# Index products of the sampled tokens as eight tiles at a time, and flags found without TensorE

## The chip, the cores and the metric

The kernel runs on one NeuronCore of a Trainium2 chip. A core has five engines that run side by side, each through its own queue in order: TensorE (PE, with weight loads shown apart as PEld), VectorE (DVE), ScalarE (ACT), GpSimd (POOL) and SyncE (SP, which issues most of the DMAs). They wait for each other through semaphores. PE writes into PSUM banks of 128 rows by 512 float32; every other working buffer lies in SBUF. The metric is the time of one execution on the device in microseconds (us).

## The reference

One decoder step for 1024 prompt positions and, beside them, 8 sampled sequences of 4 new tokens each (32 rows), which have 8192 positions in a paged cache. A projection feeds two groups of heads: sparse attention, which looks only at the 256 keys per query that an indexer picks, and retention. A gated output projection, a norm and a gated embedding follow. The change concerns the indexer:

```python
def _index_select(qi, wi, ki, qpos, kpos, topk):
    s = jnp.einsum('bqhd,bsd->bqhs', qi, ki) * (D_IDX ** -0.5)
    score = jnp.einsum('bqh,bqhs->bqs', wi, jax.nn.relu(s))
    score = jnp.where(valid, score, -jnp.inf)
    top_val, top_idx = lax.top_k(score, topk)
    return top_idx, jnp.isfinite(top_val)
```

There are 8 index heads of 64 numbers. For the sampled sequences, the keys `ki` are gathered from the cache pages; for each sequence 8192 keys meet 4 tokens x 8 heads = 32 query columns.

## The kernel before, in words

The program runs in stages: norms and index projections with the prompt's index scores (to about 186 us), the sample index stage (to about 343), four loops over pairs of heads, in which retention's projections `pqk` and `pvg` run among attention pieces (to about 690), then prompt attention, output projection, gate and embedding. The order of instructions on each engine isn't written out by hand. A planner places them, by its own estimate of when each can run, from the order of the source and from generators that other loops step.

**The sample index stage** is the loop over `b` (8 sequences) and `a` (2 halves of the pages). For each `(b, a)`, POOL gathers 128 rows of keys (`kx`, L794). PE transposes them in two halves of eight 128x128 blocks (`ptx`, L804), and ACT copies each half out of PSUM (`kT`, L805, two buffers). Two keys lie in the 128 rows of a transposed column, 64 rows each. So `qbd` holds the queries as a block diagonal matrix, 128 rows by 64 columns: rows 0 to 63 with the 32 query columns of one key and zeros, rows 64 to 127 with zeros and the same queries. Two products (L808) of 512 columns each fill one bank `pox`, and ACT writes its relu into `rl` (L811). `head_sum` multiplies four such `rl` by the head weights in four tiles of 32 columns (`py`, L767 and L770), and ACT copies it to `ys` (L772). `by_key` transposes `ys` (`pxt`, L779), and DVE copies it into the order of the keys (`xe`, L783), which a DMA stores.

PSUM in this stage has two pairs of banks ("S", for `ptx`), two banks "b" (`py` and the projection's `pb`) and two banks "t", which `pox`, `pxt`, the flag's `pfl` and others share.

**What else runs in the loop.** `unit(1.4)` steps the projection (`pb`, products L252 to L254 with 384 or 288 columns), which gives PE work between the index products. `tickb` counts steps of `bisect_prompt`, the search for the prompt's 256 best keys per query. Its counting steps use DVE (L656) and ACT (`js`, L652). Then DVE finds the largest of what remains (`lw`, L697). Then a flag tells if any row needs a further search (`anywhere`, then a branch, L706, whose body this execution's data skip), and last DVE builds the mask for six query blocks of 384 to 1024 columns (L715 to L731). `anywhere` is used a second time, with its branch at L962, by `bisect_sample`, the search for the sampled tokens, whose totals per step (`stot`, L871) PE sums from `sgn` (L909) during the loops over pairs of heads. `anywhere` sums its operand over the 128 rows with a PE product into `pfl` (L621), DVE compares the sum with zero (L623), and DVE loads it into a register (L624).

Of the kernel before, what the change touches and what calls it, by code (L numbers as in the profile page):

```python
# [10 lines left out]
F32 = mybir.dt.float32  # L11
F32R = mybir.dt.float32r
BF16 = mybir.dt.bfloat16
I32 = mybir.dt.int32
# [106 lines left out]
def tile_step(ctx: ExitStack, tc: tile.TileContext, I, O):  # L121
    nc = tc.nc
# [176 lines left out]
    xt_d = dram.tile([8, 128, 512], F32, name="xt_d")  # L299
    wi_d = dram.tile([1, 256], F32, name="wi_d")  # L300
    def load_pt():
        ptp = lp
        pti = ptp.tile([128, 2, 8], I32, name="pti")
        pt_t = I["page_table"]
        for a in range(2):
            nc.sync.dma_start(pti[a::2, 0, :], pt_t.rearrange("b n -> n b"))
        nc.sync.dma_start(pti[:, 1, :], bass.AP(tensor=pt_t.tensor, offset=pt_t.offset + 63,
                                                  ap=[[0, 128], [64, 8]]))
        ptf = ptp.tile([128, 8], F32, name="ptf")
        nc.vector.tensor_copy(ptf, pti[:, 0, :])  # L310
        lf = ptp.tile([128, 8], F32, name="lf")
        nc.vector.tensor_copy(lf, pti[:, 1, :])
        nc.vector.tensor_scalar(lastidx, lf, 128.0, C("prow"), op0=ALU.mult, op1=ALU.add)
        kf = ptp.tile([128, 8], F32, name="kf")
        nc.vector.tensor_scalar(kf, ptf, 2.0, C("half"), op0=ALU.mult, op1=ALU.add)
        for a in range(2):
            nc.vector.tensor_scalar(kidx[:, a * 8:a * 8 + 8], kf, 2.0, float(a), op0=ALU.mult, op1=ALU.add)

        bi = ptp.tile([128, 2, 8], I32, name="bi")
        nc.vector.tensor_scalar(bi[:, 1, :], kf, 64.0, None, op0=ALU.mult)  # L320
        nc.vector.tensor_scalar(bi[:, 0, :], bi[:, 1, :], 11, 11, op0=ALU.arith_shift_right, op1=ALU.arith_shift_left)
        nc.vector.tensor_tensor(bi[:, 1, :], bi[:, 1, :], bi[:, 0, :], op=ALU.bitwise_xor)
        nc.vector.tensor_copy(base, bi)
# [31 lines left out]
    score = sp_.tile([128, NSC], F32, name="score")  # L355
    sxs = ExitStack()
    sx0 = sxs.enter_context(pool("sx0"))
    qbd = sx0.tile([128, 8, 64], F32, name="qbd")
    nc.gpsimd.memset(qbd, 0.0)
    kis = sx0.tile([64, NS], F32, name="kis")  # L360
    qsn = sx0.tile([64, 8, NS], F32, name="qsn")

    def q_sample_index(j, pt):
        for o in range(2):
            s = pt[o * 64:o * 64 + 64, 256:288].rearrange("p (b t) -> p b t", b=8)
            for r in range(2):
                d = qbd[r * 64:r * 64 + 64].rearrange("p b (r t h) -> p r b t h", r=2, h=8)
                nc.vector.tensor_scalar(d[:, r, :, :, 2 * j + o], s, 0.125, None, op0=ALU.mult)
            nc.vector.tensor_scalar(qsn[:, 2 * j + o, :], pt[o * 64:o * 64 + 64, 256:288], 0.125, None, op0=ALU.mult)


# [245 lines left out]

    def anywhere(bad, sp, name):

        t = bank("pfl", "t")  # L620
        nc.tensor.matmul(t[:1, :1], bad, sp_one, start=True, stop=True)  # L621
        fl = sp.tile([1, 1], I32, name=f"fl{name}")
        nc.vector.tensor_scalar(fl, t[:1, :1], 0.0, None, op0=ALU.is_gt)  # L623
        return nc.vector.value_load(fl)  # L624

    def bisect_prompt():

# [103 lines left out]
            V.tensor_scalar(mask[:, o:o + n], gt[:, :n], -BIG, BIG, op0=ALU.mult, op1=ALU.add)  # L731
            yield

    sp_one = cp.tile([128, 1], F32, name="sp_one")
    nc.gpsimd.memset(sp_one, 1.0)
    bp = bisect_prompt()

    def step(gen, n=1):
# [37 lines left out]
    def by_key(b, ys):  # L776
        pt = bank("pxt", "t")
        for i in range(4):
            nc.tensor.transpose(pt[:, i * 128:(i + 1) * 128], ys[:, i * 128:(i + 1) * 128], ident)  # L779
        xe = sx.tile([128, 4, 4, 4, 4], F32, tag="xe", bufs=1, name="xe")  # L780
        pv = pt.rearrange("p (r i e) -> p r i e", r=4, i=4)
        for t in range(4):
            nc.vector.tensor_copy(xe[:, t].rearrange("p i r u -> p r i u"), pv[:, :, :, t * 4:t * 4 + 4])  # L783
        nc.sync.dma_start(xs_d[:, b * 256:b * 256 + 256], xe.rearrange("p t i r u -> p (t i r u)"))

    def later():
        if pend:
# [2 lines left out]
    for b in range(8):  # L790
        rls = []
        for a in range(2):
            kx = sx.tile([128, 2048], F32, tag="kx", bufs=2, name="kx")
            nc.gpsimd.indirect_dma_start(  # L794
                out=kx, out_offset=None, in_=pages,
                in_offset=bass.IndirectOffsetOnAxis(ap=kidx[:, a * 8 + b:a * 8 + b + 1], axis=0))
            for up in range(2):
                pt = pair("ptx")
                kT = sx.tile([128, 1024], F32, tag="kT", bufs=2, name="kT")
                for u2 in range(2):  # L800
                    for i in range(4):
                        r2 = up * 8 + i * 2 + u2
                        c0 = u2 * 512 + i * 128
                        nc.tensor.transpose(pt[:, c0:c0 + 128], kx[:, r2 * 128:(r2 + 1) * 128], ident)  # L804
                nc.scalar.copy(kT, pt)  # L805
                po = bank("pox", "t")
                for u2 in range(2):
                    nc.tensor.matmul(po[u2 * 64:u2 * 64 + 64, :], qbd[:, b, :], kT[:, u2 * 512:u2 * 512 + 512],  # L808
                                     start=True, stop=True)
                rl = sx.tile([128, 512], F32, tag="rl", bufs=6, name="rl")  # L810
                nc.scalar.activation(rl, po, AF.Relu)  # L811
                rls.append(rl)
            later()
            tickb[0] += 1.5
            while tickb[0] >= 1:
                tickb[0] -= 1
                step(bp)
# [983 lines left out]
```

## Time and profile before

| what | value |
|---|---|
| time, median of 3 runs | 1080.16 us (1077.92 to 1082.97) |
| the profiled execution | 1081.17 us, its span 1079.4 us |
| PE busy | 999.9 us (93% of the span) |
| DVE busy | 698.3 us (65%) |
| ACT busy | 507.2 us (47%) |
| POOL busy | 287.9 us (27%) |

The profile shows one execution. "Busy" is the time in which an engine runs an instruction. A group's row gives the line, engine, operation, output and inputs, shapes, a count, and then either busy time and mean or the shortest, median and longest. What an engine waited for is named behind its idle time with an arrow. PEclk is the share of full clock that the throttle granted to PE.

### The profile page before, as it was taken

How to read it: one execution, taken by the hardware profiler on the slowest of the kernel's cores; microseconds unless marked ns; L12 is line 12 of the kernel's file. 1: busy time of each engine (PE TensorE's matmuls, PEld its weight loads, DVE VectorE, ACT ScalarE, POOL GpSimd, SP SyncE). 2: the span in 40 equal slices, each digit the busy share in tenths (PEclk: the TensorE clock that was granted, in tenths of full speed). 3: DMA queues.
4: the chain of work that ended last, by engine and by line, in shares of the span. 5: the costliest groups of instructions: out<-in, count | busy, mean ns of one | idle time of the engine just before them, and what ended most of it. 6: DMA issues, size and time to landing. Idle time of an engine off the chain costs nothing.

```text
span 1079.4 us, 19681 instructions
## 1 busy us (share of the span) xinstructions
PE 999.9 (93%) x7375; PEld 844.5 (78%) x7375; DVE 698.3 (65%) x2012; ACT 507.2 (47%) x1094; POOL 287.9 (27%) x287
## 2 busy tenths in 40 slices
PE   3899997988999889999889996999998799999998
PEld 2899997666776788898788884566665799999998
DVE  6847768989401898978967947776763522684332
ACT  5545554986434256842523436655554332452210
POOL 3102223111201532413713521635331321122100
PEclk9999999999999889999989995999999899999999
DMA  8211235546443211202201624524211511332211
GB/s 284 67 59 50 78 95 178 173 137 204 127 158 120 58 40 39 66 18 87 71 12 42 179 85 118 148 79 118 60 45 51 154 60 40 116 126 80 89 37 41
DMA packets 98309, 102.24 MB, mean 95 GB/s; under 512 B 21347, under 2 KB 88387, under 8 KB 95907
## 3 DMA queue, kind: packets, MB, share of 16 engines
q1 hardware_dynamic: 92450, 74.74, 23.1%
q0 software_dynamic: 5760, 26.22, 7.9%
q8 instruction: 58, 0.95, 0.4%
q14 instruction: 41, 0.33, 0.1%
HBM read 79.25 MB, written 21.68 MB: 94 GB/s over the span
## 4 chain that ended last, share of the span: by engine, by line
PE 65%; DVE 13%; issue 7%; ACT 6%; DMA 6%; POOL 3%; SPq 1%; DVEq 0%; POOLq 0%; ACTq 0%
PE pb L252 4%; PE pb L253 4%; PE pb L254 4%; PE pg L262 3%; PE pg L264 3%; PE pg L263 3%; PE po L262 2%; PE po L264 2%; PE po L263 2%; PE pvg L263 2%; PE pvg L264 2%; PE pvg L262 2%; PE ob L1577 2%; PE pox L808 2%; PE ptp L1569 2%
## 5 line engine op out<-in xcount | busy, mean ns | idle before, releaser
L1144 POOL DMA_INDIRECT kvs<-in_cache_kv,idx x64 | 66.1, 1032 | 92.0 <-ACT pT L1574 29.8
L262 PE MATMUL pqk<-whi_qkb,xh 128*128 128x256 f32 x256 | 75.7, 296 | 3.7 <-DVE rp L1033 3.7
L262 PE MATMUL po<-whi_o,yTh 128*128 128x256 f32 x256 | 74.0, 290 | 4.7 <-DVE x L1664 4.1
L262 PE MATMUL pvg<-whi_vgb,xh 128*128 128x256 f32 x256 | 76.6, 299 | 1.2 <-ACT sg L1046 1.1
L263 PE MATMUL pvg<-wlo_vgb,xh 128*128 128x256 f32 x256 | 75.9, 297 | 0.0
L264 PE MATMUL pvg<-whi_vgb,xl 128*128 128x256 f32 x256 | 74.6, 291 | 0.0
L263 PE MATMUL pqk<-wlo_qkb,xh 128*128 128x256 f32 x256 | 74.5, 291 | 0.0
L264 PE MATMUL pqk<-whi_qkb,xl 128*128 128x256 f32 x256 | 74.1, 289 | 0.0
L264 PE MATMUL po<-whi_o,yTl 128*128 128x256 f32 x256 | 73.3, 288 | 0.0
L263 PE MATMUL po<-wlo_o,yTh 128*128 128x256 f32 x256 | 73.1, 286 | 0.0
L262 PE MATMUL pg<-whi_g,yTh 128*128 128x256 f32 x256 | 72.7, 284 | 0.0
L264 PE MATMUL pg<-whi_g,yTl 128*128 128x256 f32 x256 | 72.3, 282 | 0.0
L263 PE MATMUL pg<-wlo_g,yTh 128*128 128x256 f32 x256 | 72.3, 282 | 0.0
L497 DVE SCALAR_TENSOR_TENSOR score<-r,wi,score 128x384 f32<-128x384 f32 (+5 forms) x42 | 44.3, 1054 | 21.0 <-ACT r L493 19.8
L1562 ACT ACTIVATE L<-L,mn 128x128 f32<-128x128 f32 (+7 forms) x64 | 49.5, 776 | 14.1 <-DVE mn L1559 13.9
L262 PEld LDWEIGHTS pqk<-whi_qkb,xh 128*128 128x128 f32 x256 | 49.3, 193 | 7.9 <-issue 5.0
L262 PEld LDWEIGHTS po<-whi_o,yTh 128*128 128x128 f32 x256 | 49.8, 194 | 6.4 <-DVE x L1664 4.3
L1758 DVE TENSOR_TENSOR sgm<-pu,sgm 128x256 f32<-128x256 f32 x32 | 13.6, 424 | 62.3 <-PE pu L264 55.3
L262 PEld LDWEIGHTS pvg<-whi_vgb,xh 128*128 128x128 f32 x256 | 49.7, 194 | 3.1 <-ACT sg L1046 1.3
L1569 PEld LDWEIGHTS ptp<-cst,L 128*128 128x128 f32 x288 | 31.9, 142 | 24.3 <-issue 19.6
L493 ACT ACTIVATE r<-si 128x384 f32<-128x384 f32 (+5 forms) x48 | 36.3, 759 | 30.2 <-PE si L351 29.0
L264 PEld LDWEIGHTS pqk<-whi_qkb,xl 128*128 128x128 f32 x256 | 49.5, 194 | 1.1 <-issue 0.8
(540 smaller groups left out, 3288.0 us busy)
## 6 DMA issues: line engine op xcount, KB each, us to landing
wraw_qkb<-in_w_in SPq DMA_DIRECT2D x16, 256.0 KB
wraw_vgb<-in_w_in SPq DMA_DIRECT2D x16, 256.0 KB
wraw_o<-in_w_out SPq DMA_DIRECT2D x8, 512.0 KB
qas<-qas_d SPq DMA_DIRECT2D x8, 512.0 KB
xr<-in_x_prompt SPq DMA_DIRECT2D x8, 512.0 KB
wraw_g<-in_w_ple_gate SPq DMA_DIRECT2D x8, 512.0 KB
out_y_prompt<-sgm SPq DMA_DIRECT2D x32, 128.0 KB
qas_d<-qst SPq DMA_DIRECT2D x8, 384.0 KB
```

What stands on the lines that cost most here:

```text
L252: nc.tensor.matmul(pt[:m, :n], wh, xh[:, k, ts], start=(k == 0), stop=False)
L253: nc.tensor.matmul(pt[:m, :n], wh, xl[:, k, ts], start=False, stop=False)
L254: nc.tensor.matmul(pt[:m, :n], wl, xh[:, k, ts], start=False, stop=(k == KC - 1))
L262: nc.tensor.matmul(pt[:, :n], ah, hi[:, k, :n], start=(k == 0), stop=False)
L263: nc.tensor.matmul(pt[:, :n], ah, lo[:, k, :n], start=False, stop=False)
L264: nc.tensor.matmul(pt[:, :n], al, hi[:, k, :n], start=False, stop=(k == kc - 1))
L493: nc.scalar.activation(r[:, :n], s[:, :n], AF.Relu)
L497: nc.vector.scalar_tensor_tensor(sc, r[:, :n], wi[:, qb, h:h + 1], sc, op0=ALU.mult, op1=ALU.add)
L808: nc.tensor.matmul(po[u2 * 64:u2 * 64 + 64, :], qbd[:, b, :], kT[:, u2 * 512:u2 * 512 + 512], start=True, stop=True)
L1144: return nc.gpsimd.indirect_dma_start(out=dst, out_offset=None, in_=kvflat, in_offset=bass.IndirectOffsetOnAxis(ap=idx, axis=0))
L1562: behind[0] = nc.scalar.activation(L[:, :n], L[:, :n], AF.Exp, bias=least, scale=-1.0, accum_out=sm[:, i4:i4 + 1])
L1569: nc.tensor.transpose(tp[:, i4 * 128:i4 * 128 + 128], P[i4][:, kb * 128:kb * 128 + 128], ident)
```

## The change

It has five parts.

1. `qbd` keeps only the 32 query columns, once in rows 0 to 63 and once in rows 64 to 127, without the zeros. For each `(b, a)` both halves are transposed and copied first. Then eight products of 64 rows by 32 columns write two banks `pox`: `part(e, r)` takes row half `r` and column tile `e`, writes rows 32e to 32e + 31 of bank `r`, and reads half of `kT`. Product (3, 1), which needs the second `kT`, is issued first, the other seven after it. Both relus follow.
2. Since the keys stand in another order, `by_key` copies `xe` in eight pieces in place of four.
3. `tickb` advances by 2 per `(b, a)` in place of 1.5.
4. `anywhere` runs on DVE alone: the operand is put into a 32-column block, transposed in 32x32 blocks, reduced, the four results are brought into one row, reduced and loaded. The constant `sp_one` goes.
5. `load_pt` uses another pool, and the clearing of `qbd` on POOL goes.

```diff
--- before.py
+++ after.py
@@ -299,7 +299,7 @@
     xt_d = dram.tile([8, 128, 512], F32, name="xt_d")
     wi_d = dram.tile([1, 256], F32, name="wi_d")
     def load_pt():
-        ptp = lp
+        ptp = sx0
         pti = ptp.tile([128, 2, 8], I32, name="pti")
         pt_t = I["page_table"]
         for a in range(2):
@@ -355,8 +355,7 @@
     score = sp_.tile([128, NSC], F32, name="score")
     sxs = ExitStack()
     sx0 = sxs.enter_context(pool("sx0"))
-    qbd = sx0.tile([128, 8, 64], F32, name="qbd")
-    nc.gpsimd.memset(qbd, 0.0)
+    qbd = sx0.tile([128, 8, 32], F32, name="qbd")
     kis = sx0.tile([64, NS], F32, name="kis")
     qsn = sx0.tile([64, 8, NS], F32, name="qsn")
 
@@ -364,8 +363,8 @@
         for o in range(2):
             s = pt[o * 64:o * 64 + 64, 256:288].rearrange("p (b t) -> p b t", b=8)
             for r in range(2):
-                d = qbd[r * 64:r * 64 + 64].rearrange("p b (r t h) -> p r b t h", r=2, h=8)
-                nc.vector.tensor_scalar(d[:, r, :, :, 2 * j + o], s, 0.125, None, op0=ALU.mult)
+                d = qbd[r * 64:r * 64 + 64].rearrange("p b (t h) -> p b t h", h=8)
+                nc.vector.tensor_scalar(d[:, :, :, 2 * j + o], s, 0.125, None, op0=ALU.mult)
             nc.vector.tensor_scalar(qsn[:, 2 * j + o, :], pt[o * 64:o * 64 + 64, 256:288], 0.125, None, op0=ALU.mult)
 
 
@@ -617,11 +616,19 @@
 
     def anywhere(bad, sp, name):
 
-        t = bank("pfl", "t")
-        nc.tensor.matmul(t[:1, :1], bad, sp_one, start=True, stop=True)
-        fl = sp.tile([1, 1], I32, name=f"fl{name}")
-        nc.vector.tensor_scalar(fl, t[:1, :1], 0.0, None, op0=ALU.is_gt)
-        return nc.vector.value_load(fl)
+        sq = sp.tile([128, 2, 32], F32, name=f"sq{name}")
+        four = sp.tile([1, 4], F32, name=f"four{name}")
+        fl = sp.tile([1, 2], I32, name=f"fl{name}")
+        V = nc.vector
+        V.memset(sq[:, 0], 0.0)
+        V.tensor_copy(sq[:, 0, 0:1], bad)
+        V.transpose(sq[:, 1], sq[:, 0])
+        V.tensor_reduce(sq[:, 0, 1:2], sq[:, 1], axis=AX.X, op=ALU.max)
+        for i in range(4):
+            V.tensor_copy(four[:, i:i + 1], sq[32 * i:32 * i + 1, 0, 1:2])
+        V.tensor_reduce(four[:, 0:1], four, axis=AX.X, op=ALU.max)
+        V.tensor_copy(fl[:, 0:1], four[:, 0:1])
+        return V.value_load(fl[:, 0:1])
 
     def bisect_prompt():
 
@@ -731,8 +738,6 @@
             V.tensor_scalar(mask[:, o:o + n], gt[:, :n], -BIG, BIG, op0=ALU.mult, op1=ALU.add)
             yield
 
-    sp_one = cp.tile([128, 1], F32, name="sp_one")
-    nc.gpsimd.memset(sp_one, 1.0)
     bp = bisect_prompt()
 
     def step(gen, n=1):
@@ -777,11 +782,13 @@
         pt = bank("pxt", "t")
         for i in range(4):
             nc.tensor.transpose(pt[:, i * 128:(i + 1) * 128], ys[:, i * 128:(i + 1) * 128], ident)
-        xe = sx.tile([128, 4, 4, 4, 4], F32, tag="xe", bufs=1, name="xe")
-        pv = pt.rearrange("p (r i e) -> p r i e", r=4, i=4)
+        xe = sx.tile([128, 4, 2, 4, 8], F32, tag="xe", bufs=1, name="xe")
+        pv = pt.rearrange("p (i a r e) -> p i a r e", i=4, a=2, r=2)
         for t in range(4):
-            nc.vector.tensor_copy(xe[:, t].rearrange("p i r u -> p r i u"), pv[:, :, :, t * 4:t * 4 + 4])
-        nc.sync.dma_start(xs_d[:, b * 256:b * 256 + 256], xe.rearrange("p t i r u -> p (t i r u)"))
+            for a in range(2):
+                nc.vector.tensor_copy(xe[:, t, a].rearrange("p e (i r) -> p e i r", r=2),
+                                      pv[:, :, a, :, t * 4:t * 4 + 4].rearrange("p i r e -> p e i r"))
+        nc.sync.dma_start(xs_d[:, b * 256:b * 256 + 256], xe.rearrange("p t a e u -> p (t a e u)"))
 
     def later():
         if pend:
@@ -794,24 +801,32 @@
             nc.gpsimd.indirect_dma_start(
                 out=kx, out_offset=None, in_=pages,
                 in_offset=bass.IndirectOffsetOnAxis(ap=kidx[:, a * 8 + b:a * 8 + b + 1], axis=0))
+            kTs = []
             for up in range(2):
                 pt = pair("ptx")
                 kT = sx.tile([128, 1024], F32, tag="kT", bufs=2, name="kT")
-                for u2 in range(2):
-                    for i in range(4):
-                        r2 = up * 8 + i * 2 + u2
-                        c0 = u2 * 512 + i * 128
-                        nc.tensor.transpose(pt[:, c0:c0 + 128], kx[:, r2 * 128:(r2 + 1) * 128], ident)
+                for i in range(8):
+                    r2 = up * 8 + i
+                    nc.tensor.transpose(pt[:, i * 128:i * 128 + 128], kx[:, r2 * 128:(r2 + 1) * 128], ident)
                 nc.scalar.copy(kT, pt)
-                po = bank("pox", "t")
-                for u2 in range(2):
-                    nc.tensor.matmul(po[u2 * 64:u2 * 64 + 64, :], qbd[:, b, :], kT[:, u2 * 512:u2 * 512 + 512],
-                                     start=True, stop=True)
+                kTs.append(kT)
+            po = [bank("pox", "t") for _ in range(2)]
+
+            def part(e, r):
+                rr = slice(64 * r, 64 * r + 64)
+                return nc.tensor.matmul(po[r][32 * e:32 * e + 32, :], qbd[rr, b, :],
+                                        kTs[e // 2][rr, e % 2 * 512:e % 2 * 512 + 512], start=True, stop=True)
+
+            first = part(3, 1)
+            with tc.issue_after(first.ins):
+                for e, r in ((3, 0), (2, 1), (2, 0), (1, 1), (1, 0), (0, 1), (0, 0)):
+                    part(e, r)
+            for r in range(2):
                 rl = sx.tile([128, 512], F32, tag="rl", bufs=6, name="rl")
-                nc.scalar.activation(rl, po, AF.Relu)
+                nc.scalar.activation(rl, po[r], AF.Relu)
                 rls.append(rl)
             later()
-            tickb[0] += 1.5
+            tickb[0] += 2
             while tickb[0] >= 1:
                 tickb[0] -= 1
                 step(bp)
```

Three places show what the planner makes of it. First PE at the end of the sample index stage, where no projection is left to put between. `ptx` are the transposes, `pox` the index products, `pxt` and `py` the two steps of the head sums; x8 counts products. Before:

```order
L808 MATMUL pox<-kT,qbd 64x512 x2
L804 MATMUL ptx<-cst,kx 128x128 x14
L779 MATMUL pxt<-cst,ys 128x128 x4
L767 MATMUL py<-rl,wst 32x512
L770 MATMUL py<-rl,wst 32x512 x3
L808 MATMUL pox<-kT,qbd 64x512 x2
L804 MATMUL ptx<-cst,kx 128x128 x13
L808 MATMUL pox<-kT,qbd 64x512 x2
L804 MATMUL ptx<-cst,kx 128x128 x3
L808 MATMUL pox<-kT,qbd 64x512 x4
```

With the change:

```order
L817 MATMUL pox<-kT,qbd 32x512 x8
L810 MATMUL ptx<-cst,kx 128x128 x11
L784 MATMUL pxt<-cst,ys 128x128 x4
L772 MATMUL py<-rl,wst 32x512
L775 MATMUL py<-rl,wst 32x512 x3
L810 MATMUL ptx<-cst,kx 128x128 x8
L817 MATMUL pox<-kT,qbd 32x512 x8
L810 MATMUL ptx<-cst,kx 128x128 x8
L817 MATMUL pox<-kT,qbd 32x512 x8
```

The two or four products that stood after each half of the transposes now stand as eight after both halves. Earlier in the stage the same eight stand among the projection's products, and between `pxt` of b=3 and the next eight lie 12 transposes, `py` and 20 products of the projection; ahead of `pxt` of b=2 lie 19 products of the projection more than before.

Second, DVE from the last `MAX` of the prompt's search to its branch. Before, the copies `xe` of five sequences (x20) and the start of the first pair of heads (`sh_qk`, `rp`) stand between:

```order
L697 MAX top<-mask 128x8
L698 SCALAR_TENSOR_TENSOR ge<-need,top 128x6
L702 TENSOR_TENSOR pick<-pick,top 128x48
L699 TENSOR_REDUCE cf<-ge 128x1
L703 TENSOR_REDUCE v<-pick 128x6
L783 COPY xe<-pxt 128x4x4x4 x20
L879 MEMSET ssm 128x1
```

With the change:

```order
L709 TENSOR_TENSOR pick<-pick,top 128x48
L706 TENSOR_REDUCE cf<-ge 128x1
L710 TENSOR_REDUCE v<-pick 128x6
L624 COPY sqp<-cf 128x1
L625 STREAM_TRANSPOSE sqp<-sqp 128x32
L626 TENSOR_REDUCE sqp<-sqp 128x1
L628 COPY fourp<-sqp 1x1 x4
L629 TENSOR_REDUCE fourp<-fourp 1x1
L630 CAST flp<-fourp 1x1
L631 TENSOR_LOAD flp
L713 COMPARE_AND_BRANCH
```

The flag and the branch follow directly, and all of the mask's 44 instructions behind them (in its order the last counting step stands one step earlier against the copies of b=1, and the copies of b=2 stand just ahead of the last `MAX`).

Third, DVE in the mask building. Before, it stands in the first pair of heads, among the rotations `rp` of the retention projections and the counts `jv` of the sampled tokens' search:

```order
L724 TENSOR_SCALAR gt,cnt<-score,tbits 128x512
L728 SCALAR_TENSOR_TENSOR rk<-eq 128x512
L1031 TENSOR_TENSOR rp_3_3871<-pqk,cst 128x256
L1032 TENSOR_TENSOR rp_3_3872<-pqk,cst 128x4x32
L1033 TENSOR_TENSOR rp_3_3872<-pqk,cst 128x4x32
L905 TENSOR_SCALAR jv,c_3736<-su_3403,ssm 128x704
L726 TENSOR_SCALAR need<-cnt 128x1
```

With the change it stands in the sample index stage:

```order
L737 TENSOR_TENSOR gt<-gt,eq 128x640
L738 TENSOR_SCALAR mask<-gt 128x640
L734 TENSOR_SCALAR eq<-score,tbits 128x768
L731 TENSOR_SCALAR gt,cnt<-score,tbits 128x768
L735 SCALAR_TENSOR_TENSOR rk<-eq 128x768
L733 TENSOR_SCALAR need<-cnt 128x1
L789 COPY xe<-pxt 128x32 x8
L736 SCALAR_TENSOR_TENSOR eq<-rk,need,eq 128x768
L737 TENSOR_TENSOR gt<-gt,eq 128x768
```

Only one sequence's copies (`xe`, b=3) stand inside the mask, behind 27 of its instructions; those of b=4 to 7 stand behind the last. In the first pair of heads DVE has the rotations and the sample search without the mask, and PE runs all products of `pqk` before the first `stot`.

## The prediction

> **What bounds the kernel now.** I began with the table of stretches, which gives each engine's busy time and the granted clock, because a mean over the span hides stages with different limits.
>
> ```profile
> core 0: us, PE busy (x) PEld busy (x) DVE busy (x) ACT busy (x) POOL busy (x), PEclk, DMA share, GB/s
> 190.00:205.00 15.00, 14.75 (x80) 8.53 (x77) 13.18 (x38) 14.96 (x27) 1.87 (x2) 0.88 0.65 218
> 220.00:240.00 20.00, 17.39 (x107) 12.37 (x108) 17.73 (x55) 17.15 (x29) 0.60 (x2) 1.00 0.31 103
> 240.00:255.00 15.00, 11.91 (x73) 7.68 (x72) 12.69 (x33) 11.78 (x20) 6.14 (x4) 1.00 0.86 265
> 255.00:335.00 80.00, 80.00 (x496) 60.00 (x494) 26.54 (x66) 36.39 (x54) 11.88 (x12) 1.00 0.42 139
> ...
> 345.00:400.00 55.00, 46.96 (x336) 43.30 (x335) 46.37 (x106) 21.91 (x39) 23.23 (x27) 0.88 0.28 67
> ...
> 490.00:560.00 70.00, 61.22 (x478) 55.08 (x476) 62.77 (x162) 24.53 (x65) 33.01 (x35) 0.95 0.20 56
> ```
>
> The sample index stage runs from about 186 to 343 us, and it has two halves. Up to 255 no engine alone sets the pace: ACT fills 14.96 of 15 us at the start, later PE has 3 us gaps, with DMA at 0.86. From 255 on PE is busy 80.00 of 80 at full clock while DVE does 26.54: only there is a microsecond less on PE a microsecond less of the stage. The next stretch, the first pair of heads (345 to 400), is the reverse: PE loses 8.0 us and part of its clock, and DVE is the full engine. 490 to 560 looks the same: PE loses 8.8 us, DVE works 62.77 of 70.
>
> **The products.** The next rows are single instructions and groups on PE: four 32-column tiles of py, a group of the products (pox), transposes, two 64-row products of retention, and neighbours of the projection (pb).
>
> ```profile
> 255.05 0.34 PE L254 MATMUL pb<-xh,wlo_ga 128*128 128x384 f32 x1
> 255.22 0.34 PE L252 MATMUL pb<-xh,whi_ga 128*128 128x384 f32 x1
> ...
> 333.01 0.63 PE L770 MATMUL py<-rl,wst 128*32 128x512 f32 x3
> ...
> 333.46 0.61 PE L770 MATMUL py<-rl,wst 128*32 128x512 f32 x3
> 334.00 1.08 PE L808 MATMUL pox<-kT,qbd 128*64 128x512 f32 x4
> 335.01 1.64 PE L804 MATMUL ptx<-cst,kx 128*128 128x128 f32 x13
> ...
> 378.93 0.37 PE L1062 MATMUL second<-qkT 64*128 64x128 f32 x1
> 378.93 0.37 PE L1062 MATMUL ret<-qkT 64*128 64x128 f32 x1
> ```
>
> One pox group (two products, four records because a float32 product takes two passes) holds PE 1.08 us. The four column tiles of py start together, and both passes are over at 334.07, 1.07 us after their start: column tiles run side by side. The two L1062 products read different halves of the rows and start at the same 378.93: row halves run side by side too. So eight tiles of 64 rows by 32 columns, which replace two pox groups, should take about 1.07 us for 2.15. No row shows both splits at once. The bounds are 1.07 (all together), 2.15 (the row halves one after the other, nothing gained) and 3.4 (only pairs together: four pairs of two passes of 0.43). I take 1.07, since each split alone appears.
>
> The Trainium skill, "TensorE: Matmul & The Clock Gate", section Part 3 (packing small matmuls), gives the span of a pack as one matmul's time plus about 4 ns per further tile; for eight tiles that is an estimate of 1.1 us, and the sum would stay as it is. No run here shows eight tiles yet, so this only supports the low end.
>
> How many groups count? This is the table of stretches for L808 alone, and two groups on ACT:
>
> ```profile
> 255.00:343.00 88.00, 20.28 (x76) 3.85 (x76) 1.00 0.39 131
> ...
> L805 ACT COPY kT<-ptx x32: 995/1016/1053, 188.1 to 338.2; 128x1024 f32<-128x1024 f32 x32
> ...
> L811 ACT ACTIVATE rl<-pox x32: 576/599/659, 191.3 to 340.4; 128x512 f32<-128x512 f32 x32
> ```
>
> 76 records are 19 of the 32 groups. Halved, 20.28 becomes 10.14: **−10.1 us**. The other 13 groups stand before 255, where ACT, DMA and waits pace the stage; I count them at nothing (cover: ACT's 14.96 of 15; if it were gone, up to 13 x 0.54 = 7 us more). At the tail nothing covers the new form: the last set needs two kT copies where one sufficed (1.02 us), and its two relus follow each other (0.60): **+1.6**.
>
> **The wait that the change adds.** All eight tiles write two banks of the tag "t", and there are only two. pxt, the transposed head sums, holds one of them until DVE has made the copies xe. Hence every pox group behind a pxt on PE's queue waits for DVE, and everything behind that pox, in order, waits too. Before, a free second bank let pox go on. That mattered little while DVE idled from 281 on:
>
> ```profile
> 259.11 0.16 DVE L660 SCALAR_TENSOR_TENSOR cnt<-cnt,cst 128x2 f32<-128x2 f32 x1 [0.19 <-ACT js L652]
> ...
> 268.17 0.61 DVE L783 COPY xe<-pxt 128x64 f32<-128x64 f32 x4
> ...
> 278.83 1.23 DVE L697 MAX8 top<-mask 128x8 f32<-128x1024 uint16 x1
> ...
> 291.86 0.62 DVE L783 COPY xe<-pxt 128x64 f32<-128x64 f32 x4 [11.25 <-PE pxt L779]
> ...
> 348.32 0.13 DVE L623 TENSOR_SCALAR flp<-pfl 1x1 int32<-1x1 f32 x1
> 354.75 0.17 DVE L715 CAST gb<-v 128x6 int32<-128x6 f32 x1 [6.30 <-DVEq L706]
> ```
>
> Now the flag, the branch and the mask building come into that idle time, and the new order puts the copies of the fourth sample row (b=3) inside the mask, behind 27 of its 44 instructions, and those of b=4 behind all. The mask costs, by groups between 345 and 420:
>
> ```profile
> L728 DVE TENSOR_TENSOR_SCAN rk<-eq 128x384 f32<-128x384 bf16 (+5 forms) x6 | 12.3, 2055 | 0.0
> ...
> L729 DVE SCALAR_TENSOR_TENSOR eq<-rk,need,eq 128x384 bf16<-128x384 f32 (+5 forms) x6 | 5.9, 986 | 0.0
> L724 DVE TENSOR_SCALAR_CACHE_REDUCE gt<-score,tbits 128x384 bf16<-128x384 f32 (+5 forms) x6 | 5.6, 937 | 0.0
> L727 DVE TENSOR_SCALAR eq<-score,tbits 128x384 bf16<-128x384 f32 (+5 forms) x6 | 3.7, 614 | 0.0
> L730 DVE TENSOR_TENSOR gt<-gt,eq 128x384 bf16<-128x384 bf16 (+5 forms) x6 | 3.7, 611 | 0.0
> ...
> L731 DVE TENSOR_SCALAR mask<-gt 128x384 bf16<-128x384 bf16 (+5 forms) x6 | 2.0, 338 | 0.0
> ```
>
> Together 33.2 us over six widths (384 to 1024, 4224 columns). The first 27 instructions are three whole widths (1536 columns) and most of the fourth's first steps: about 16 us; the rest 17.
>
> DVE's timetable in the changed kernel: its order ends the bisection about one step (4.2 us) earlier against the copies of b=1, so the last MAX ends near 277 instead of 280. The flag takes eleven small DVE instructions instead of a PE product and one compare; by rows like L660's 0.16 that is 1.9 us (bounds 0.6 and 3). Load and branch cost 6.3 us of idle DVE before; I take 5, since the DMA stands at 0.42 there (255 to 335) and not as full as just after 345, with 0 and 6.3 as bounds. So the mask begins near 284.5, and xe of b=3 is ready at about 284.5 + 16 + 1.2 = 302 (eight half-size copies taken as twice the four's 0.61).
>
> PE's timetable: pxt of b=2 comes some 2.5 us later than before (19 more pb products at 0.17 ahead of it, one group less), 270; the pox behind it would go at 276.5, when DVE has just freed the bank. By the order's count pxt of b=3 then stands at 289.5, and the next pox follows after 12 transposes (0.126 each), py and 20 pb products: 296. PE waits **6 us**. The copies of b=4 end near 320.5, PE asks near 320: **1 us**. A stall of this size is followed by a slower clock, as the rows in the next part show: **2.5**. Hold together **+9.5**, between 0 (branch without idle time) and 16.
>
> **The first pair of heads and later.** PE's waits from 345 to 440, then short stretches in the columns of the first table (0.76 in the first is the granted clock):
>
> ```profile
> PE stot L871 <- DVE sgn L909: 3.1, 2, 2.8
> PE pqk L262 <- DVE rp L1033: 2.6, 3, 2.2
> PE ret L1052 <- POOL qk L1036: 2.6, 1, 2.6
> ...
> 365.00:370.00 5.00, 2.16 (x12) 1.55 (x10) 4.31 (x9) 3.96 (x6) 3.83 (x5) 0.76 0.00 0
> 370.00:375.00 5.00, 5.00 (x24) 4.66 (x24) 5.00 (x16) 0.00 (x0) 1.73 (x4) 0.56 0.00 0
> ...
> 390.00:395.00 5.00, 3.20 (x10) 2.30 (x10) 4.90 (x12) 2.70 (x8) 1.23 (x3) 0.65 0.00 0
> 395.00:400.00 5.00, 5.00 (x31) 5.00 (x31) 4.94 (x12) 3.27 (x6) 0.00 (x0) 0.67 0.00 0
> ...
> 550.00:560.00 10.00, 10.00 (x67) 10.00 (x66) 6.74 (x34) 3.40 (x13) 0.44 (x1) 0.73 0.04 7
> ```
>
> Idle 8.0 plus busy time at a lower clock (2.16 x 0.24 + 5 x 0.44 + 3.2 x 0.35 + 5 x 0.33 = 5.5) make 13.5 us of loss. 33 us of mask and 6.3 of branch leave this stretch, so the 2.2 wait for rp behind the branch should go, and sgn comes earlier. What is late next is sgn for the first stot: PE's new order runs all pqk products and then waits for it, and two long passes over Xt (DMA) lie ahead. I take half: **−6.5**, bounds 0 and −13.5. From 490 to 560 the loss is 8.8 idle and 2.7 of clock; the sample search may begin earlier, but its own chain remains. I take a quarter, **−3**, bounds +5 (another order) and −11.5.
>
> "TensorE: Matmul & The Clock Gate" of the Trainium skill, section Part 1 (the HAM clock gate), lets the clock fall only after about 3.4 us of idle PE. Here a 2.6 us wait was followed by 0.56 (370 to 375), so the rows disagree, and they decide; by the rule the 1 us stall would cost no clock and the 6 us one would, which is what the sum has.
>
> **The sum**, against the profiled execution (1081.17, span 1079.4, 1.8 around it; 1.0 above the median of 1080.16, inside the runs' 1077.92 to 1082.97): −10.1 + 1.6 + 9.5 − 6.5 − 3 = −8.5, that is **1073 us**.
>
> **Rivals.**
> - *No hold.* If the branch costs DVE little, xe is on time: 9.5 less, 1063. For it: other copies waited on PE, 11.25 us at 291.86. Against it: the 6.30 row of this very branch. Chance 0.20. With most of the DVE relief realised as well (another 9): 1054, 0.07.
> - *The hold grows (the slower side).* The bisection does not end earlier (+4.2 on DVE), and the branch costs its 6.3 and the flag 3 (+2.4): xe of b=3 is 6.6 later, stalls for b=3 and b=4 make 14 with clock dips of 5, and relief later on is eaten by the late sample search: −10.1 + 1.6 + 19 − 4 = +6.5, 1088. Each microsecond past 296 at which DVE frees the bank costs one; it ends slower once the hold exceeds about 17 us with a relief of 4. For it: DVE is in order and has no slack there. Against: ACT's second half has slack, 36.39 of 80. Chance 0.12.
> - *The row halves follow each other* (2.15 us): the 10.1 is lost, the later PE shortens the hold by 6: 1078; in pairs, 3.4 us, it is 1090. Against: the rows at 378.93. Chance 0.08.
> - *The relief is worth nothing*: the losses from 345 on belong to the sample search and DMA, not to the mask: 1082. For it: the stot wait is a chain of its own. Chance 0.11.
>
> **How the numbers follow.** My forecast has 0.42. About 0.5% (5.4 us) is what can be told from no change: faster is below 1074.8, slower above 1085.6. The forecast straddles the first (0.28 faster, 0.14 same); no hold gives 0.27 faster; the hold 0.02 same and 0.10 slower; the row halves 0.01, 0.05 and 0.02; no relief 0.00, 0.09 and 0.02. Sum: faster 0.56, same 0.30, slower 0.14. The range, 1054 to 1087, runs from full relief to the edge of the grown hold; the forecast's own is 1066 to 1080.
>
> **What would show it.** Right: pox sets of about 1.1 us; PE idle before a pox near 296 to 302 with xe as releaser, DVE in the mask then, and a dip of the clock behind; from 345 on DVE well under 46 of 55. Wrong: pox sets above 2 us; no PE wait on xe; PE losses after the stage as large as before; or a gain before 255.

## The result, and the profile after

The change made the kernel slower: 1088.12 us (median of 4 runs, 1087.61 to 1089.05) against 1080.31 beside it, a ratio of 1.0073 with a 95% interval of 1.0048 to 1.0098. The profiled execution took 1089.05 us with a span of 1087.3, 7.9 longer than the 1079.4 before.

The table of stretches of the changed kernel, in the stretches that were read of the kernel before:

```profile
core 0: us, PE busy (x) PEld busy (x) DVE busy (x) ACT busy (x) POOL busy (x), PEclk, DMA share, GB/s
190.00:205.00 15.00, 12.90 (x89) 7.73 (x88) 11.92 (x36) 13.52 (x22) 1.87 (x2) 0.76 0.54 183
220.00:240.00 20.00, 15.80 (x91) 9.12 (x90) 17.03 (x58) 12.77 (x23) 0.94 (x1) 0.74 0.41 137
240.00:255.00 15.00, 12.79 (x95) 11.38 (x97) 12.60 (x30) 12.67 (x21) 6.63 (x4) 1.00 0.53 157
255.00:335.00 80.00, 73.36 (x530) 57.88 (x523) 62.02 (x143) 34.76 (x54) 12.66 (x9) 0.91 0.43 143
345.00:400.00 55.00, 47.97 (x379) 41.32 (x380) 28.09 (x95) 27.07 (x49) 22.37 (x35) 0.91 0.29 74
490.00:560.00 70.00, 65.71 (x532) 58.77 (x532) 60.07 (x167) 24.09 (x68) 33.93 (x34) 0.98 0.24 66
```

Three things stand out. From 255 to 335, DVE went from 26.54 to 62.02 us of 80 and PE from 80.00 to 73.36: the mask is in the stage, and PE waits there. From 345 to 400, DVE fell from 46.37 to 28.09. And in the early half, which was to stay as it was, the clock of 220 to 240 is 0.74 instead of 1.00.

Equal pieces of work show where the time went. These are PE's rows for `py` of the third sequence and for the first product of the pairs of heads, in the kernel before and then in the changed one (start, duration):

```profile
253.60 0.62 PE L767 MATMUL py<-rl,wst 128*32 128x512 f32 x1
...
343.43 1.07 PE L271 MATMUL pqk<-wraw_qkb,xs 128*32 128x256 f32 x16
```

```profile
260.62 1.06 PE L772 MATMUL py<-rl,wst 128*32 128x512 f32 x1
...
353.26 1.94 PE L271 MATMUL pqk<-wraw_qkb,xs 128*32 128x256 f32 x16
```

| from, to | before | after | difference |
|---|---|---|---|
| start, `py` of the third sequence | 253.6 | 260.6 | +7.0 |
| from there to the first `pqk` | 89.8 | 92.6 | +2.8 |
| from there to the first `pvg` (377.9; 383.2) | 34.5 | 29.9 | −4.6 |
| from there to the end of the span | 701.5 | 704.1 | +2.6 |

The four differences add up to +7.8, which is the span's difference but for rounding. So the early half lost most, the late half and the time after the first pair of heads lost a little each, and the first pair gained.

**In the late half the predicted wait came, seven microseconds later.** PE's rows in the changed kernel, the sets of eight among the projection:

```profile
292.00 1.09 PE L817 MATMUL pox<-kT,qbd 64*32 64x512 f32 x16
...
296.86 0.60 PE L784 MATMUL pxt<-cst,ys 128*128 128x128 f32 x4
...
303.39 1.04 PE L817 MATMUL pox<-kT,qbd 64*32 64x512 f32 x2
309.37 1.95 PE L817 MATMUL pox<-kT,qbd 64*32 64x512 f32 x14 [4.94 <-DVE xe L789]
```

A set (16 records) takes 1.09 us at full clock, as a group of two did. The first product of the next set fills the free bank, and the rest waits 4.94 us for `xe`. The last row is 1.95 us long: the clock was 0.67 from 310 to 315. DVE's rows of that time, in which the copies come behind 27 instructions of the mask:

```profile
284.71 0.14 DVE L630 CAST flp<-fourp 1x1 int32<-1x1 f32 x1
289.01 0.17 DVE L722 CAST gb<-v 128x6 int32<-128x6 f32 x1 [4.17 <-DVEq L713]
...
308.31 0.13 DVE L733 TENSOR_SCALAR need<-cnt 128x1 f32<-128x1 f32 x1
308.36 0.86 DVE L789 COPY xe<-pxt 128x32 f32<-128x32 f32 x8
```

**The early half.** The waits of PE from 204 to 262 us by what ended them (total, times, longest), before and after:

```profile
PE kvt L405 <- ACT kvs L401: 2.9, 1, 2.9
PE pox L808 <- DVE vnew L411: 1.6, 1, 1.6
PE pxt L779 <- ACT rl L811: 1.1, 1, 1.1
PE kvt L405 <- DVE xe L783: 0.7, 1, 0.7
PE ptx L804 <- ACT kT L805: 0.4, 2, 0.3
```

```profile
PE kvt L404 <- ACT kvs L400: 3.9, 2, 3.1
PE ptx L810 <- ACT kT L811: 2.8, 2, 1.7
PE pox L817 <- DVE vnew L410: 2.2, 1, 2.2
```

The waits grew by some 2 us in all, far less than 7. What changed more is the clock. Two stretches of the kernel before, and the same of the changed one:

```profile
204.00:233.00 29.00, 25.29 (x159) 18.94 (x158) 26.30 (x83) 23.77 (x42) 1.87 (x2) 1.00 0.49 162
...
233.00:262.00 29.00, 25.91 (x160) 19.57 (x159) 25.80 (x68) 22.75 (x38) 6.62 (x4) 1.00 0.50 157
```

```profile
204.00:233.00 29.00, 24.05 (x146) 17.87 (x146) 25.68 (x78) 21.86 (x40) 1.87 (x2) 0.85 0.46 152
...
233.00:262.00 29.00, 25.09 (x165) 18.16 (x163) 24.25 (x78) 23.00 (x38) 6.63 (x4) 0.85 0.53 167
```

0.15 of the 49.1 busy microseconds, 7.4, went to the slower clock there. The 2 and the 7.4 do not add up to 7.0, because the stretches hold different work and the new products save PE time in them.

Where do the longer waits come from? Two of them fit the form of the sets. A set needs both `kT` buffers, so the next transposes wait for `kT` (2.8 us where 0.4 stood). It also needs both banks "t", and `kvt`, the transposed new keys and values of the prompt, takes such a bank, which DVE empties only between the counting steps (`pox` for `vnew`, 2.2 where 1.6 stood). The longest wait, 3.1 us of `kvt` for `kvs`, is neither a bank nor a buffer of the set. These are ACT's rows there, before and then after:

```profile
221.31 0.40 ACT L401 COPY kvs<-pb 128x288 f32<-128x288 f32 x1 [1.68 <-DMA out_k_prompt<-kvs]
```

```profile
223.05 1.15 ACT L659 ACTIVATE js<-mask,cand 128x1024 bf16<-128x1024 bf16 x1 [1.88 <-DVE cand L684]
...
224.20 0.76 ACT L400 COPY kvs<-pb 128x288 f32<-128x288 f32 x2
```

With the change the copy `kvs` stands on ACT's queue behind a counting piece `js`, which itself waits 1.88 us for DVE; in the kernel before, the copy waited for a DMA. So this wait comes from DVE's counting, by way of ACT's queue, and not from the products' banks.

### The profile page after: what moved, and what is told of

It is laid out like the page before. It is cut to its first block, busy times and chain, and to the rows that moved or that the text cites. A ratio compares the mean times of both kernels' runs of the same rounds, so it can differ in the third digit from the quotient of the medians.

```text
span 1087.3 us, 19979 instructions
## 1 busy us (share of the span) xinstructions
PE 996.1 (92%) x7499; PEld 846.3 (78%) x7499; DVE 705.1 (65%) x2062; ACT 501.5 (46%) x1090; POOL 288.8 (27%) x285
## 4 chain that ended last, share of the span: by engine, by line
PE 46%; DVE 11%; issue 5%; DMA 4%; POOL 3%; ACT 3%; SPq 1%; DVEq 0%; POOLq 0%; ACTq 0%
PE pg L262 3%; PE pg L264 3%; PE pg L263 3%; PE pvg L262 3%; PE po L264 3%; PE po L262 3%; PE po L263 3%; PE ob L1592 3%; PE pvg L263 2%; PE pvg L264 2%; PE ptp L1584 2%; DMA wraw_vgb<-in_w_in 1%; PE sa L1568 1%; PE pty L1639 1%; POOL kvs L1159 1%
## 5 line engine op out<-in xcount | busy, mean ns | idle before, releaser
L264 PEld LDWEIGHTS pqk<-whi_qkb,xl 128*128 128x128 f32 x256 | 49.1, 192 | 2.7 <-issue 2.4
L263 PEld LDWEIGHTS po<-wlo_o,yTh 128*128 128x128 f32 x256 | 50.2, 196 | 0.5 <-issue 0.4
```

What stands on the lines that cost most here:

```text
L263: nc.tensor.matmul(pt[:, :n], ah, lo[:, k, :n], start=False, stop=False)
L264: nc.tensor.matmul(pt[:, :n], al, hi[:, k, :n], start=False, stop=(k == kc - 1))
```

## The experiments

Two theories at first. A: the sets of eight lose by themselves, in the early half, since PE then waits more for buffers and banks. B: the mask in the stage is what costs. The results first, each against the runs of the kernel before beside it; the last two columns are starts and differences of starts in each profile, as in the table above. Each profile is one execution, and in the experiments the executions of one kernel differ by 7 to 16 us in total:

| run | median us | ratio, 95% interval | `py` of the third | from there to `pqk` |
|---|---|---|---|---|
| before | 1080.1 to 1081.2 | 1 | 253.6 | 89.8 |
| the change | 1088.12 | 1.0073 (1.0048 to 1.0098) | 260.6 | 92.6 |
| products only | 1085.84 | 1.0044 (1.0018 to 1.0070) | 259.6 | 84.4 |
| flag only | 1077.23 | 0.9965 (0.9927 to 1.0002) | 251.5 | 91.8 |
| two steps only | 1083.01 | 1.0029 (1.0008 to 1.0050) | 252.6 | 90.4 |
| change, three `kT` | 1082.91 | 1.0008 (0.9982 to 1.0034) | 260.2 | 88.7 |
| change, `pxt` in "b" | 1082.74 | 1.0015 (0.9994 to 1.0035) | 257.1 | 91.5 |
| change, `kvt` and `pxt` in "b" | 1077.02 | 0.9988 (0.9960 to 1.0015) | 257.1 | 84.4 |
| these two in "b" and three `kT` | 1082.20 | 1.0031 (1.0003 to 1.0060) | 258.9 | 85.7 |
| change, `xe` on ACT | 1084.98 | 1.0037 (1.0016 to 1.0057) | 258.4 | 89.7 |
| change, `xe` and `kvt` on ACT | 1082.30 | 1.0026 (1.0003 to 1.0049) | 258.5 | 87.8 |
| sets from b=3 on | 1076.82 | 0.9967 (0.9934 to 1.0000) | 250.5 | 84.9 |
| sets from b=3 on, flag on DVE, `xe` on ACT | 1075.91 | 0.9953 (0.9920 to 0.9987) | 254.8 | 86.8 |
| sets up to b=2 | 1087.15 | 1.0055 (1.0036 to 1.0074) | 262.8 | 89.9 |

**Products only.** The new products and `by_key`, with the flag and the steps as before:

```diff
-        sq = sp.tile([128, 2, 32], F32, name=f"sq{name}")
...
+        t = bank("pfl", "t")
+        nc.tensor.matmul(t[:1, :1], bad, sp_one, start=True, stop=True)
...
-            tickb[0] += 2
+            tickb[0] += 1.5
```

> The change with the flag found by the product on PE as before and with 1.5 steps per half (parts 1, 2 and 5 alone); by its order the mask then stays in the first pair of heads. Theory A, the products in sets of eight cost time themselves, because a set holds both buffers of kT until it has run and PE's transposes wait: about the loss seen up to the third py (7 us) remains, the second half gains some 8, no wait of pox for xe, tail +2; no relief for the first pair of heads. Total 1080 to 1086, and py of the third sequence 5 to 7 us later than before. Theory B, the products gain and only the mask in front of the copies xe loses: about 1070, third py no later than before.

The early loss is there without any mask in the stage (259.6), the late half is 5.4 us shorter where 8 was expected, and the whole is slower by 0.44%. Theory A is right that the sets lose by themselves, and B does not explain the loss alone; whether the `kT` buffers are the way, this run does not show.

**Flag only.** The old products, with the prompt's flag on DVE:

```diff
+        if name == "s":
+            t = bank("pfl", "t")
...
+        w = sp.tile([128, T], BF16, tag="jk", bufs=1, name="jkf").bitcast(F32)
+        sq = w[:, :64].rearrange("p (a b) -> p a b", a=2)
```

> The kernel before with only the prompt's flag found on DVE (its scratch laid into a buffer that is there already; the sampled tokens' flag stays on PE). By its order branch and mask then stand in the sample index stage, with the old products, which take one bank of the tag t at a time. Theory A: the second bank lets pox go on while xe waits, so the stage ends within 2 us of before, and the first pair of heads gains what the change showed there, 4 to 5 us: 1074 to 1077. Theory B, the mask in the stage is what costs: 1084 or more, with PE waits for xe in the stage.

The stage is no longer than before (91.8 + 251.5 = 343.3). The waits of PE from 255 to 345 show why: with one bank per group, the copies behind the mask cost 1.5 us and not 4.94.

```profile
PE pox L823 <- DVE xe L798: 1.5, 1, 1.5
PE pxt L794 <- ACT ys L787: 0.7, 1, 0.7
```

The first pair of heads gained 2.9 us and not 4 to 5, and the total lies 0.2 us above the expected range. The whole is 0.35% faster, with an interval that just reaches no change.

**Two steps only.** The kernel before with one line changed, which also brings the mask into the stage:

```diff
-            tickb[0] += 1.5
+            tickb[0] += 2
```

> The kernel before with two steps of the prompt's search per half in place of 1.5 and nothing else: the flag is still summed on PE, but by its order branch and mask stand in the sample index stage, with the old products. If the gain of the flag on DVE is only that the mask leaves the first pair of heads, this gains as much: 1074 to 1079. If the flag's place on PE matters (PE's branch or the product waits), 1080 or more.

The stage ends as before (343.1), but the whole is 0.29% slower. So moving the mask out of the first pair of heads is not a gain in itself. With the flag on DVE the stretch from 343 to 400 had PE at 51.92 us, here at 47.88. Here the profiled execution was a long one of its kernel (1088.08 us, median 1083.01), there a short one (1074.52, median 1077.23), so part of that difference may be scatter; the rest was not found.

**Three buffers for `kT`**, paid with one for `ys`:

```diff
-                kT = sx.tile([128, 1024], F32, tag="kT", bufs=2, name="kT")
+                kT = sx.tile([128, 1024], F32, tag="kT", bufs=3, name="kT")
...
-        ys = sx.tile([128, 512], F32, tag="ys", bufs=2, name="ys")
+        ys = sx.tile([128, 512], F32, tag="ys", bufs=1, name="ys")
```

> The change with three buffers for kT in place of two, paid with one buffer in place of two for ys. Theory A: the waits of ptx for kT (6.0 us up to 255) mostly go and one of the half-clock stretches with them; the first pqk of the pairs of heads starts 3 to 6 us earlier, total 1082 to 1085. Theory B: nothing moves by more than 1 us, 1087 to 1089. One buffer for ys may give back up to 1 us.

The total and the first `pqk` (348.9, 4.3 us earlier) came as theory A expected, but not by its way: the third `py` stays at 260.2, with the clock at 0.84 and 0.85 in the two stretches, and the gain lies behind it. From 186 to 256 PE's waits of `ptx` for `kT` are 7.1 us, where the change has 6.0: they did not go. A third `kT` buffer does not take the early loss away.

**`pxt` in a bank "b".**

```diff
-        pt = bank("pxt", "t")
+        pt = bank("pxt")
```

> The change with the transposed head sums pxt in a bank of the tag b (shared with pb and py) in place of t, so that pox does not wait for xe. If the hold by the copies xe in the mask is worth the 4.9 us wait and the slower clock behind it (2 to 3 us), and pb does not take over the wait: 1080 to 1083. If the wait moves to pb, which needs a bank b every 3 to 4 us: 1086 to 1092, with PE waits of pb for xe.

The total is in the range for the hold's going, though 3.6 of the 4.7 us that the stage gained lie before the third `py`; the late half is 1.1 us shorter. The wait had moved: `pb` now waits 4.3 us for DVE in the mask.

**`kvt` and `pxt` in banks "b".** The edit above and:

```diff
-        tp = bank("kvt", "t")
+        tp = bank("kvt")
```

> The change with kvt (the transposed new keys and values, which DVE copies out among the counting steps) and pxt in banks of the tag b, so that the tag t holds nothing that waits for DVE. Theory T (sets of eight need both banks t, and whatever DVE holds of them stops PE, in both halves of the stage): third py 3 to 6 us earlier than with the change (255 to 258), no wait of pox for a DVE copy, first pqk before 347, total 1077 to 1082. Theory S (the early loss lies in the order of the sets or in the two buffers kT, not in the banks): third py at 259 to 261 as with a third kT buffer, total 1082 to 1086. If the waits only move to pb: PE waits of pb for DVE of 3 us or more.

The total falls to 1077.02, by the ratio 0.12% under the kernel before, which is no difference that can be told. The stage ends at 341.5. The clock in the early stretches is 1.00 and 0.94:

```profile
204.00:233.00 29.00, 24.82 (x213) 18.90 (x211) 25.19 (x81) 25.39 (x45) 3.75 (x4) 1.00 0.51 164
233.00:262.00 29.00, 24.83 (x176) 20.93 (x176) 24.24 (x74) 24.13 (x40) 7.48 (x5) 0.94 0.63 200
```

Theory T is right in its direction: 3.6 of the 7 us are gone, though as many as with `pxt` alone. And the order changed with the banks: the wait of `kvt` for `kvs`, 3.1 us with the change, is 0.5 here from 204 to 262, so the run does not show the banks' part alone. Other waits moved, as the third alternative said. PE's waits for DVE now stand before `pb` and `py` (186 to 256, then 256 to 350):

```profile
PE pb L252 <- DVE cand L684: 3.1, 1, 3.1
PE pb L252 <- DVE knew L410: 1.9, 1, 1.9
```

```profile
PE py L772 <- DVE xe L789: 3.7, 1, 3.7
```

**The same with three `kT` buffers** (both edits together):

> The change with kvt and pxt in banks b and with three buffers for kT (one for ys): both suspects of the early half at once. If banks and buffers together make the early loss, third py at 252 to 255 and total 1073 to 1077; if the rest of it lies elsewhere (order, ACT), third py stays at 256 to 258 and the total at 1076 to 1080.

It missed the total: 1082.20, and the third `py` at 258.9. So a third buffer does not take the rest away; with one `ys` the wait of `py` for `xe` even grew to 7.0.

**`xe` on ACT**, and then **`kvt`'s copies on ACT too**:

```diff
-                nc.vector.tensor_copy(xe[:, t, a].rearrange("p e (i r) -> p e i r", r=2),
+                nc.scalar.copy(xe[:, t, a].rearrange("p e (i r) -> p e i r", r=2),
...
-        nc.vector.tensor_copy(st[:, 1, :nb], tp[:, :nb])
+        nc.scalar.copy(st[:, 1, :nb], tp[:, :nb])
...
-            nc.vector.tensor_copy(new, tp[:NS, 256:384])
+            nc.scalar.copy(new, tp[:NS, 256:384])
```

> The change with the copies xe on ACT in place of DVE; banks as in the change. Both theories: the wait of pox behind the mask (4.9 us) goes and the half clock behind it, the early half stays: third py at 259 to 261, first pqk 4 to 7 us earlier than with the change, total 1080 to 1084.

> As the one before, and the copies out of kvt on ACT too, so that no bank t waits for DVE; the banks are those of the change. Theory T: third py at 254 to 258, total 1076 to 1081. Theory S: third py at 259 or later (ACT has more work there), total 1081 to 1085.

With `xe` on ACT the hold is gone: from 295 to 315 PE is busy throughout at full clock.

```profile
295.00:315.00 20.00, 20.00 (x164) 15.84 (x163) 19.62 (x30) 10.62 (x28) 4.99 (x4) 1.00 0.47 154
```

The first `pqk` comes 5.2 us earlier, as expected; the third `py` (258.4) was 0.6 us below its range and the total 1 us above. With `kvt` on ACT as well, the third `py` stays at 258.5 and the clock of 204 to 233 at 0.83: `pox` still waits for `vnew`, now 2.7 us for ACT, and `kvt` for `kvs` 2.8 us. So DVE's holding of the banks is not the only thing. The third `py` lies between the two theories' ranges; the total is theory S's.

**Sets from b=3 on.** The old products for the first three sequences, sets for the others, flag and steps as before; a set reads its 32 columns from the block diagonal matrix:

```diff
+            if b < SETS:
...
+            else:
+                kTs = []
...
+                    return nc.tensor.matmul(po[r][32 * e:32 * e + 32, :], qbd[rr, b, 32 * r:32 * r + 32],
```

> The kernel before with the sets of eight tiles only for the sequences b=3 to 7 (the block diagonal matrix stays; a set reads the 32 columns of it that belong to its row half), the flag on PE and 1.5 steps as before, so that the mask stays in the first pair of heads. Theory E (in the early half, where kvt, DVE's counting and ACT pace the stage, sets of eight lose 5 to 7 us; in the late half, where PE is the bound, they gain 5 to 6): third py at 251 to 255 as before, from there to the first pqk 84 to 86 us in place of 89.8, total 1073 to 1077. If the early loss is not tied to where the sets run: third py at 257 or later, total 1080 or more.

Both halves came as theory E said: 250.5, then 84.9. The whole is 0.33% faster, with an interval that just reaches no change. These are its PE rows:

```profile
250.50 0.62 PE L768 MATMUL py<-rl,wst 128*32 128x512 f32 x1 [0.53 <-ACT rl L822]
...
335.36 1.94 PE L271 MATMUL pqk<-wraw_qkb,xs 128*32 128x256 f32 x16
```

**The same with the flag on DVE and `xe` on ACT**, so with the mask in the late half:

> As the one before, with the prompt's flag found on DVE, so that branch and mask stand in the late half, and the copies xe on ACT, so that no bank waits for the mask. Theory E: third py at 251 to 255, to the first pqk 84 to 88 us, total 1071 to 1077. If the mask in the stage costs without any bank waiting for it: 3 us or more longer from the third py to the first pqk than without it.

At 1075.91 us it has the lowest median of the study: 0.47% under the kernel before, with an interval that excludes no change (0.9920 to 0.9987), and by the medians 1.1% under the change. From the run before it and from the flag alone it can't be told apart, since their intervals overlap. The late half is 1.9 us longer than without the mask, less than the 3 that would have told against it. In the early half, with the old products, the clock of 204 to 233 is 0.88 here, behind a wait of `kvt` of 3.0 us, and the third `py` comes 4.3 us later than in the run before it.

**Sets up to b=2**, the counterpart (the conditions `b < SETS` become `b >= SETS`):

> The counterpart of the late sets: sets of eight only for the sequences b=0 to 2, the old products from b=3 on, flag on PE, 1.5 steps, the mask in the first pair of heads. Theory E: third py at 257 to 261, from there to the first pqk 88 to 91 us as before, total 1083 to 1088. If the early loss needs the later sets (it comes from the planner's order as a whole): third py at 251 to 255, total 1078 to 1082.

262.8, even later than expected, then 89.9 as before, and 0.55% slower. Its rows:

```profile
262.77 0.62 PE L768 MATMUL py<-rl,wst 128*32 128x512 f32 x1
...
352.62 1.07 PE L271 MATMUL pqk<-wraw_qkb,xs 128*32 128x256 f32 x16
```

The pair shows the place: the same sets lose 9.2 us in the early half and gain 4.9 in the late one. The loss is larger than the 4.3 us by which the third `py` differs among the kernels with the old products there.

## Why the prediction was wrong

The forecast was 1073 us, with a chance of 0.14 for slower and an upper end of 1087; the time lies 1.1 us above that end. Step by step, with the prediction's term and what was measured:

- **The price of a set, 1.07 us: right.** 1.09 us for sixteen records at full clock, which excludes the rivals of 2.15 and 3.4 us. The Trainium skill's span of a pack ("TensorE: Matmul & The Clock Gate", Part 3) agrees: the estimate from it was 1.1. The totals given for the two rivals were 1.2 us too high by their own terms: 1072.7 + 10.1 − 6 is 1076.8, not 1078.
- **"The other 13 groups stand before 255 ...; I count them at nothing": this is the step that failed.** They cost 7.0 us. I had given this step bounds on the gain's side only (0 to 7 us more). That an engine which does not pace a stretch gains nothing by less work may stand; that its new order and form (both banks, both buffers, in one set) can add waits for the others, and a slower clock behind them, was left out. The clock took 7.4 us and the waits grew by 2. Of the banks, I had priced `xe` alone, although `kvt` takes a bank "t" too and waits for the same DVE, which was busy 17.73 of 20 us; and that ACT's copies would stand differently among the counting steps I had not looked at. The sets of the first three sequences alone reproduce the loss.
- **The late half, −10.1 + 1.6 + 9.5 = +1.0: right in kind, +2.8 measured.** The wait was 4.94 us where 6 was said, the branch 4.17 where 5 was said; the wait for b=4 did not come, and the clock behind the hold took 1.9 (0.63 x 0.35 from 305 to 310 and 5.00 x 0.33 from 310 to 315), so the hold cost 6.8 where 9.5 was counted. That the wait came out so near is in part luck. The last `MAX` ended 5.8 us later than forecast, and the first 27 instructions of the mask took 19.4 us in place of 16; PE happened to be 7.4 us late as well. Without the hold, the late half gains 4.9 to 5.4, and not the 8.5 of −10.1 + 1.6: the tail lost more than was counted. In the late sets the last 10.4 us of the stage have 3.4 us idle and a clock of 0.67, in the kernel before 1.0 us idle and 1.00, which makes 2.5 + 2.3 = 4.8 where 1.6 was counted.
- **The first pair of heads, −6.5: −4.6 measured, but not shown to be the mask's going.** The run of two steps also takes the mask away and gains nothing there.
- **Later, −3: the change lost 2.6 from there on.** Between kernels that differ only in the stage, the time from the first `pqk` to the end scatters from 728 to 743 us in the profiles (before: 736.0). The planner sets the later order anew for each, and executions of one kernel differ by 7 us and more; no run separates the two. A term of −3 can't be seen in that, and had no ground.

The rival of the slower side named a resource that may have a part, the banks "t" held by DVE, and nearly the right total (1088), but for another place: it needed the waits behind the mask to grow to 14 us, and they were 4.9. The loss was in the half that it did not look at, so that its total came near by luck.

How the early loss divides is not settled. In the five profiles with the old products there, the third `py` starts at 250.5 to 254.8; in the nine with sets, at 257.1 to 262.8, without overlap. Seven of the nine show a clock of 0.83 to 0.88 from 204 to 233 us, but so does one of the five (0.88, at 254.8). The two with `kvt` and `pxt` out of the tag "t" keep it at 1.00 there and still start at 257.1 and 258.9, with waits of `pb` for DVE in its place. So the slower clock is a large part where it occurs, and not the whole; the waits for DVE and ACT change their place with the banks and with the planner's order, and no run took them all away or changed the order or the clock by itself. That the sets lose in the early half is shown; by which of these ways is not.

## What to carry to other kernels

An instruction group that does the work of two in the time of one also needs the inputs and outputs of two at once. Count what else uses those banks and buffers, and which engine releases them, in every stretch where the group runs, and look at what the new order puts ahead of them on the other engines' queues. A stretch where PE is not the bound can lose, and here the form paid only where PE was the bound. When a planner orders the queues, measure equal pieces of work in both traces before arguing from totals.

## What the runs showed of the hardware

The clock fell after short waits, and not after all of them, and the length of one wait did not decide it. A wait of 2.86 us (before, `kvt` at 221.8) left it at 1.00 from 204 to 233. One of 3.12 us (after, the same place) was followed by 0.72 from 218 to 233, and one of 2.21 us (after, `pox` at 254.7) by 0.50 from 256 to 262:

```profile
218.00:233.00 15.00, 10.80 (x57) 6.96 (x56) 12.32 (x38) 9.58 (x18) 0.94 (x1) 0.72 0.51 170
...
256.00:262.00 6.00, 4.30 (x24) 2.62 (x20) 4.11 (x19) 4.74 (x8) 0.00 (x0) 0.50 0.72 243
```

At the same place, 0.26 us more of a wait went with 3.0 us of busy time lost to the clock (10.80 x 0.28).

Two of DVE's mask instructions took 2.34 and 2.62 us, while POOL ran two products of 4.76 us together (from 292.28). With `pxt` in "b" the same two had ended before POOL's pair began, and took 0.26 and 0.48 us. No run tests whether POOL is the cause. The rows are from the changed kernel:

```profile
292.45 2.34 DVE L738 TENSOR_SCALAR mask<-gt 128x384 bf16<-128x384 bf16 x1
294.72 2.62 DVE L734 TENSOR_SCALAR eq<-score,tbits 128x512 bf16<-128x512 f32 x1
```

The idle time of DVE at the prompt's branch was 6.30 to 8.08 us in the four kernels where the branch stands behind the stage, and 1.37 to 5.77 us in the ten where it stands in it. Among these it was 4.17 with the change and 1.52 with the flag alone; what sets it was not found.
